# One more chunk of product g by seven small products, and a new table for the planner

## The chip, the cores and the metric

The kernel runs on one core of one Trainium2 chip. The metric is the device time of one execution in microseconds (us), the median of several runs. The kernel before takes 757.42 us (757.23 to 758.36, three runs).

## What is computed

One layer of a gated short-convolution mixer, all in float32: 1024 frames of 1024 features, an inner width of 2048. Cut to what matters:

```
u = rms_norm(x, pre_norm)
z, bg, cg, v = split(u @ w_in, 4)          # w_in 1024 x 8192
y = bg * causal_dwconv(cg * v, conv_w) * silu(z)      # 3 taps along the frames
out = x + rms_norm(y @ w_out, post_norm)   # w_out 2048 x 1024
```

Nearly all arithmetic is in the two matrix products.

## The kernel before, in words

**Tiles.** A float32 product is done as three float32r matmuls: an operand is split into a high and a low part, and lo x hi, hi x lo and hi x hi are summed in PSUM. The high part is a cast on ACT (names ending in h: wch, dwf1h), the low part a subtraction on VectorE (wcl, dwf1l), so each weight tile costs one operation on either. In the trace VectorE is DVE, ScalarE ACT, GpSimd POOL, SyncE SP.

**First product.** The 2048 inner columns go in 16 chunks c, and each chunk in two column pairs: p = 2c holds cg and v, p = 2c + 1 holds z and bg. A pair is multiplied by Strassen and Winograd's scheme with seven products a, b, c, e, d, f, g in place of eight; one is 4 x 3 matmuls of 128 x 512. POOL and VectorE form the sums of weight blocks that it needs (se, sc, sf, raw); the products gather in PSUM banks px, pv, py, from which ACT and VectorE take partial results (sna, snc, sne).

**Second level.** In the middle chunks the products b, f and g of both pairs together are done by the same scheme once more: seven small ones, a' to g', of 2 x 3 matmuls of 128 x 256 each (`deep_product`, L1472). Their weights are dwb, dwf, dwg with sums dsb, dsf, dsg; their results gather in banks px2b, pv2b, px2f, px2g and so on, and are added over by VectorE (for g: gs, then px). The left operands are u_g and others, made from u once. The second level of g overwrites a part of u_g; `restore_u` (L1723) reads that part from memory and splits it again, behind the last chunk that uses the second level.

**Which chunks.** `by_seven(z, c)` (L822) answers whether product z of chunk c is done by seven small ones: from chunk 2 up to but not including LAST[z] (L820), which was 16 for b, 15 for f and 14 for g. `late_conv(c)` (L946) follows from it: where g is done by seven, the convolution's last steps of chunk c (cv, then y, written out for the second product, and the sums s of it) are left for chunk c + 1.

**Second product.** y (y_d in memory), its sums (s_d) and w_out with its sums (t_d, tb_d) are multiplied in the same way from about 603 us on (names starting with o). Behind it stand the norm and the store.

**Order.** TensorE works in the order in which the code issues its matmuls. All other engines' order is made by a planner when the kernel is built: the class Plan records every operation, `deadlines` (L375) gives each a latest time, worked back from the matmul that needs it with an assumed length for each operation, and `arrange` (L428) plays the engines through and takes on each the ready operation with the earliest latest time; an idle VectorE may take an addition that was POOL's. PLAN (L28) holds the constants, and under "boost" a table that moves the latest time of single operations by their number. On the chip each engine then runs its row in that order and waits at the first operation whose input is missing.

Of the kernel before, what the change touches and what calls it, by code (L numbers as in the profile page):

```python
# [26 lines left out]
)  # L27
PLAN = {  # L28
    "end": 14.0,
    "psum": 3.0,  # L30
    "store": 6.0,
    "turns": 1,
    "apart": 11.0,
    "hard": 2.0,
    "lock": 0.3,
    "sum": 10.0,
    "early": 0.0,
    "gap": 0.5,
    "least": 1.0,
    "free": 40.0,  # L40
    "take": 11.0,
    "held": {"snc_1": 1.95},
    "ahead": {"sync": 24.0, "gpsimd": 18.0, "scalar": 11.0, "vector": 11.0},
    "busy": {"vector": 1.9, "scalar": 0.3, "gpsimd": -2.1},
    "slack": {"tensor": 1.0, "gpsimd": 0.8, "sync": 1.0, "scalar": 0.1, "vector": 0.1},
    "boost": {
# [38 lines left out]
    },  # L85
}
BY_BANK_DEEP = (("b", 0), ("b", 1), ("b", 2), ("f", 0), ("f", 2))
# [2 lines left out]
class View:  # L90
# [3 lines left out]
    def __init__(self, tile, steps, ids, dtype):  # L94
        self.tile, self.steps, self.ids, self.dtype = tile, steps, ids, dtype
# [111 lines left out]
    ((1, 2, 5, 6), 192),  # L207
)
LOW_PAGES = (3, 10, 11, 13, 15, 16, 5, 6, 8, 9)
U_SLOTS = (5, 4, 2, 6, 1, 3, 0, 0, 5, 2, 6, 4, 1, 3, 0, 5, 2, 6, 4, 1, 6, 3, 0, 4, 2, 5, 6, 1, 0, 3, 2, 4, 5, 6, 0, 4, 1, 5, 3, 6, 0, 2)  # L210


def gap(ctx, tc, name, size):
# [5 lines left out]
class Shelves:  # L219

    def __init__(self, ctx, tc):
        self.at, self.slots = {}, list(U_SLOTS)
        for n, (slots, room) in enumerate(U_LAYOUT):
            pool = ctx.enter_context(tc.tile_pool(name=f"up{n}", bufs=1))
            self.at.update({s: pool for s in slots})
            if n == 0:
                self.low = ctx.enter_context(tc.tile_pool(name="low_pages", bufs=1))
            gap(ctx, tc, f"room{n}", room)

    def tile(self, shape, dtype, tag, **kw):  # L230
        s = self.slots.pop(0)
        return self.at[s].tile(shape, dtype, tag=f"u{s}", **dict(kw, bufs=1))


# [19 lines left out]
class Plan:  # L254
# [35 lines left out]
    def call(self, engine, where, name, args, kw):  # L290
# [3 lines left out]
        op = Op()  # L294
# [26 lines left out]
        n = max([v.ids.size for v in (outs if where == "tensor" else outs + ins)], default=1)  # L321
        psum = any(v.tile.space == "psum" for v in outs + ins)
        two = sum(v.ids.size > 1 for v in ins) > 1
        if "dma" in name:
            op.dur, op.lat = self.ISSUE[where], 3.5 if where == "sync" else 7.5
            way = 2.0 if "accum_op" in kw else 1.5 if all(v.tile.space == "dram" for v in outs + ins) else 1.0
            op.move = n * 128 * 4 * way / 310e3
        elif where == "tensor":
            op.dur, op.lat = n / 2400 + 0.0135, n / 2400 + 0.2
        elif where == "vector":  # L330
            op.dur = 0.1 + n / 960 * (1 if psum or two else 0.55)
            op.lock = n > 8 and not psum
            op.lat = op.dur + 0.1
        elif where == "scalar":
            op.dur = 0.1 + n / 1200
            op.lat = op.dur + 0.16
        else:
            op.dur = 0.16 + n / 460 if n > 8 else 0.1
            op.lock = n > 8
            op.lat = op.dur + 0.1  # L340
# [328 lines left out]
def kernel(  # L669
# [22 lines left out]
    NC = CI // P  # L692
# [18 lines left out]
    psum = plan.pool(ctx.enter_context(tc.tile_pool(name="psum", bufs=8, space=bass.MemoryType.PSUM)), 8, "psum")  # L711
# [105 lines left out]
        wt[p, i] = [page(f"w{i}{h}_{p}", F32R) for h in "hl"]  # L817
        nc.scalar.copy(wt[p, i][0], source(p, i))

    LAST = {"b": NC, "f": NC - 1, "g": NC - 2}  # L820

    def by_seven(z, c):  # L822

        return {"b": DEEP, "f": DEEP_F, "g": DEEP_G}[z] <= c < LAST[z]

# [231 lines left out]
    xb = up.tile([P, TH, D], F32, tag="u", name="xb")  # L1057
# [724 lines left out]
    for n, slot in enumerate(slots):  # L1782
        if slot[2:]:
            z, i, c = slot
            deep_product(z, c, i)
            if (i, c) == ("e'", LAST[z] - 1) and LAST[z] < NC:
                restore_u(z)
# [25 lines left out]
        ahead = DEEP <= (p - (i == "a")) // 2 < DEEP_F and (i, p % 2) in (("d", 1), ("a", 0))  # L1813
# [320 lines left out]
```

## Time and profile before

| what | value |
|---|---|
| median of three runs | 757.42 us |
| the profiled execution | 758.85 us |
| its span in the trace | 757.1 us |
| first product, steady chunks | about 35.6 us each |
| first product ends, second product begins | 603.7 us |
| last matmul | about 750 us |

The profiled execution is 1.75 us longer than the span that the trace shows, and 1.4 us over the median. All L292 in the trace is one helper line through which every planned operation is issued (L356 after the change), so groups are told apart by their tiles: `wcl<-sc,wch` is the low part of weight c, made from sum sc and the high part.

### The profile page before, as it was taken

To read this page: it belongs to the slowest core of one execution; us is meant where nothing else is said; L and a number is where in the kernel's file an instruction comes from. 1 tells how busy PE (TensorE), PEld (TensorE's weight loads), DVE (VectorE), ACT (ScalarE), POOL (GpSimd) and SP (SyncE) were. 2 spreads that over 40 slices of the span, in tenths; PEclk is the share of its full clock that TensorE was granted. 3 is DMA by queue.
4 is the path that set the end of the run, shared out by engine and by line. 5 is a ranking of instruction groups with operands and counts; after the bars stand their busy time and mean duration, and the time that the engine had idled before them with its cause. 6 is when DMAs were issued, how large, how long until landed. Compare 5 with 4: busy or idle time off the path is not lost.

```text
span 757.1 us, 12810 instructions
## 1 busy us (share of the span) xinstructions
PE 745.2 (98%) x4320; PEld 660.0 (87%) x4320; DVE 677.9 (90%) x1022; ACT 458.7 (61%) x880; POOL 462.4 (61%) x416
## 2 busy tenths in 40 slices
PE   8999999999999999999999999999999999999996
PEld 7888889999999999989998988899888889889885
DVE  6899988999998988999999999898999999877994
ACT  7765588675656564655556565666553666565831
POOL 2509997889686777697788777685739100600421
PEclk9999999999999999999999999999999999999999
DMA  9313325244333548476949383928465999566842
GB/s 313 78 49 91 111 77 162 102 142 133 98 119 98 177 115 224 111 193 163 264 119 273 95 239 80 270 95 217 118 183 179 339 362 309 201 226 206 283 149 111
DMA packets 117137, 130.11 MB, mean 172 GB/s; under 512 B 7320, under 2 KB 74704, under 8 KB 116944
## 3 DMA queue, kind: packets, MB, share of 16 engines
q1 hardware_dynamic: 112560, 120.77, 50.1%
q0 software_dynamic: 4352, 8.39, 7.2%
q8 instruction: 34, 0.56, 0.3%
q14 instruction: 31, 0.25, 0.1%
q10 hardware_dynamic: 160, 0.14, 0.1%
HBM read 101.74 MB, written 44.30 MB: 193 GB/s over the span
## 4 chain that ended last, share of the span: by engine, by line
PE 75%; DVE 8%; POOL 6%; issue 4%; DMA 3%; ACT 3%; SPq 0%; POOLq 0%; DVEq 0%; ACTq 0%
PE px L292 29%; PE pv L292 12%; PE po_x L292 8%; PE px2b L292 4%; PE po_v L292 3%; PE pp L292 3%; PE px2f L292 3%; PE px2g L292 2%; PE pv2f L292 2%; PE pv2b L292 2%; PE pb_x L292 1%; POOL dsb L292 1%; DMA raw<-in_sc_w_in 1%; PE py L292 1%; PE py2b L292 1%
## 5 line engine op out<-in xcount | busy, mean ns | idle before, releaser
L292 PE MATMUL px<-u_a,wah 128*128 128x512 f32 x248 | 75.1, 383 | 0.0
L292 PE MATMUL px<-u_c,wch 128*128 128x512 f32 x248 | 74.9, 382 | 0.0
L292 PE MATMUL px<-u_d,wdh 128*128 128x512 f32 x248 | 74.9, 382 | 0.0
L292 PE MATMUL pv<-u_e,weh 128*128 128x512 f32 x248 | 74.7, 381 | 0.0
L292 ACT COPY beside<-raw 128x512 f32<-128x512 f32 x67 | 39.6, 591 | 34.2 <-DVE dwf2l L292 9.9
L292 PEld LDWEIGHTS px<-u_a,wah 128*128 128x128 f32 x248 | 46.5, 188 | 8.0
L292 PEld LDWEIGHTS px<-u_c,wch 128*128 128x128 f32 x248 | 46.5, 188 | 7.9
L292 PEld LDWEIGHTS pv<-u_e,weh 128*128 128x128 f32 x248 | 46.5, 188 | 7.7
L292 PEld LDWEIGHTS px<-u_d,wdh 128*128 128x128 f32 x248 | 46.5, 188 | 7.6
L292 DVE SCALAR_TENSOR_TENSOR cv<-gpad,cw,cv 128x1024 f32<-128x1024 f32 x32 | 49.8, 1557 | 3.3 <-ACT cv L292 3.2
L292 POOL TENSOR_TENSOR sf<-raw,sc 128x512 f32<-128x512 f32 x30 | 44.5, 1484 | 7.1 <-DVE sc L292 5.5
L292 PE MATMUL px<-u_c,wcl 128*128 128x512 f32 x124 | 47.9, 386 | 0.2 <-DVE wcl L292 0.2
L292 PE MATMUL px<-u_a,wal 128*128 128x512 f32 x124 | 47.8, 385 | 0.0
L292 PE MATMUL px<-u_d,wdl 128*128 128x512 f32 x124 | 47.7, 385 | 0.0
L292 PE MATMUL pv<-u_e,wel 128*128 128x512 f32 x124 | 47.5, 383 | 0.0
L292 POOL TENSOR_TENSOR sc<-se,raw 128x512 f32<-128x512 f32 x25 | 35.9, 1434 | 19.0 <-DVE se L292 10.4
L292 POOL TENSOR_TENSOR rs_post<-ve_post,minus_half 128x1 f32<-128x1 f32 x7 | 6.5, 941 | 65.9 <-DVE ve_post L292 65.9
L292 POOL TENSOR_TENSOR raw<-raw,raw 128x512 f32<-128x512 f32 x31 | 43.5, 1403 | 4.2 <-DVE se L292 3.8
L292 POOL TENSOR_TENSOR se<-raw,raw 128x512 f32<-128x512 f32 x22 | 32.2, 1463 | 18.7 <-DMA raw<-in_sc_w_in 9.4
L292 ACT COPY sna<-px 128x512 f32<-128x512 f32 x30 | 17.6, 585 | 34.4 <-PE px L292 34.4
L292 DVE TENSOR_TENSOR wcl<-sc,wch 128x512 fp32r<-128x512 f32 x31 | 33.8, 1089 | 5.0 <-ACT wch L292 5.0
L292 DVE TENSOR_TENSOR wel<-se,weh 128x512 fp32r<-128x512 f32 x31 | 32.3, 1043 | 0.0
(486 smaller groups left out, 2615.8 us busy)
## 6 DMA issues: line engine op xcount, KB each, us to landing
raw<-in_sc_w_in SPq DMA_DIRECT2D x128, 256.0 KB, 5.2
y_d<-cv SPq DMA_DIRECT2D x16, 512.0 KB, 2.7
s_d<-s SPq DMA_DIRECT2D x32, 256.0 KB, 4.9
t_d<-in_sc_w_out POOLq DMA_DIRECT2D x16, 512.0 KB, 8.5
tb<-in_sc_w_out SPq DMA_DIRECT2D x16, 256.0 KB, 3.5
t_d<-in_sc_w_out SPq DMA_DIRECT2D x16, 256.0 KB, 4.9
t_d<-t_d SPq DMA_DIRECT2D x16, 256.0 KB, 4.6
s<-y_d SPq DMA_DIRECT2D x16, 256.0 KB, 4.6
```

The source lines that it names most:

```text
L292: getattr(engine, name)(*(self.plain(a) for a in args), **{k: self.plain(a) for k, a in kw.items()})
```

## The change

**The product.** LAST["g"] goes from 14 to 15. Chunk 14's product g is no longer 2 x 12 matmuls of 512 columns but 7 x 6 of 256; `restore_u("g")` and the last plain g move a chunk on, and `late_conv(14)` becomes true.

**The planner.** Its assumed length of a matmul goes from n / 2400 + 0.0135 us to n / 2400 + 0.0088 for 512 columns and + 0.0079 for 256. Nine constants of PLAN and the boost table are new; with one more product by seven the operations of chunk 14 and behind it also have other numbers.

**Slots.** The memory slots of the u tiles, before a list in order of use, are now looked up by name; they are the same slots.

```diff
 PLAN = {
-    "psum": 3.0,
+    "psum": 2.53,
...
-    "apart": 11.0,
+    "apart": 10.4,
...
-    "sum": 10.0,
+    "sum": 9.37,
...
-    "gap": 0.5,
-    "least": 1.0,
+    "gap": 0.97,
+    "least": 0.35,
...
-    "take": 11.0,
+    "take": 9.19,
...
-    "ahead": {"sync": 24.0, "gpsimd": 18.0, "scalar": 11.0, "vector": 11.0},
+    "ahead": {"sync": 25.43, "gpsimd": 18.27, "scalar": 11.0, "vector": 9.92},
...
-    "slack": {"tensor": 1.0, "gpsimd": 0.8, "sync": 1.0, "scalar": 0.1, "vector": 0.1},
+    "slack": {"tensor": 0.96, "gpsimd": 0.75, "sync": 1.0, "scalar": 0.1, "vector": 0.1},
     "boost": {
-        0: -1.88, 1: 31.37, 2: -1.93, 4: 16.59, 5: 18.27, 6: 0.14, 20: 0.84, 21: 1.2, 22: 10.67, 27: -0.09,
...
+        0: -1.88, 1: 31.93, 2: -0.45, 4: 16.59, 5: 18.27, 6: 0.14, 20: 0.84, 22: 10.67, 23: 0.68, 26: 1.31,
...
-U_SLOTS = (5, 4, 2, 6, 1, 3, 0, 0, 5, 2, 6, 4, 1, 3, 0, 5, 2, 6, 4, 1, 6, 3, 0, 4, 2, 5, 6, 1, 0, 3, 2, 4, 5, 6, 0, 4, 1, 5, 3, 6, 0, 2)
+U_SLOTS = {
+    "u_a": 5, "u_b": 4, "u_c": 2, "u_e": 6, "u_d": 1, "u_f": 3, "xb": 0, "u_g": 0, "ou_a0": 5, "oy_a0": 2,
...
-        self.at, self.slots = {}, list(U_SLOTS)
+        self.at = {}
...
-        s = self.slots.pop(0)
+        s = U_SLOTS[kw["name"]]
...
         elif where == "tensor":
-            op.dur, op.lat = n / 2400 + 0.0135, n / 2400 + 0.2
+            op.dur = n / 2400 + (0.0088 if n == 512 else 0.0079 if n == 256 else 0.0135)
+            op.lat = n / 2400 + 0.2
         elif where == "vector":
...
-    LAST = {"b": NC, "f": NC - 1, "g": NC - 2}
+    LAST = {"b": NC, "f": NC - 1, "g": NC - 1}
```

The order that the planner makes differs from row 81 us on, on all four engines; VectorE has 8 rows more, ACT 5, POOL 1, and a number of additions have changed between POOL and VectorE. Three places follow. Numbers in names are of single tiles and differ between the two programs.

**First place: VectorE in chunk 14**, about 544 to 551 us before. s_13 is a sum of y of chunk 13, sna, snc and sne are partial results. Before:

```order
L292 TENSOR_TENSOR s_13_6276<-cv_6384,s_13_6276 128x512
L292 TENSOR_TENSOR cv_6384<-cv_6384,sna_6067 128x512
L292 TENSOR_TENSOR sne_6426<-px_6278,sne_6426 128x512
L292 SCALAR_TENSOR_TENSOR s_13_6365<-s_13_6276,s_13_6365 128x512
L292 TENSOR_TENSOR u_g<-ug,u_g 128x2x256
L292 SCALAR_TENSOR_TENSOR s_13_6522<-cv_6384,s_13_6365 128x512
L292 TENSOR_TENSOR snc_6396<-px2f_6461,snc_6396 128x256
L292 TENSOR_TENSOR wcl_6537<-sc_6391,wch_6441 128x512
L292 TENSOR_TENSOR snc_6396<-pv_6389,snc_6396 128x512
L292 TENSOR_TENSOR dwf1l_6553<-dsf_14_6477,dwf1h_6518 128x512
```

After:

```order
L356 TENSOR_TENSOR s_13_6342<-cv_6377,s_13_6342 128x512
L356 TENSOR_TENSOR wcl_6479<-sc_6370,wch_6410 128x512
L356 TENSOR_TENSOR sne_6424<-px_6279,sne_6424 128x512
L356 TENSOR_TENSOR snc_6388<-px2f_6458,snc_6388 128x256
L356 TENSOR_TENSOR dwf1l_6503<-dsf_14_6398,dwf1h_6485 128x512
L356 TENSOR_TENSOR snc_6388<-pv_6386,snc_6388 128x512
L356 TENSOR_TENSOR wel_6522<-se_6335,weh_6448 128x512
L356 SCALAR_TENSOR_TENSOR s_13_6481<-s_13_6342,s_13_6481 128x512
L356 TENSOR_TENSOR sna_6318<-px2b_6417,sna_6318 128x256
L356 SCALAR_TENSOR_TENSOR s_13_6546<-cv_6377,s_13_6481 128x512
```

The split u_g is gone from here (it stands 40 rows on, in chunk 15); wcl has moved up to the row behind the first product with s_13, and the two longer operations on s_13 (SCALAR_TENSOR_TENSOR) have moved behind dwf1l and wel.

**Second place: POOL in chunk 8**, about 319 to 331 us before. dsf_8 is a sum for the small products of f; its first half comes from one sf tile, its second from another; t and tb are sums of w_out. Before:

```order
L292 TENSOR_TENSOR dsb_8_3745<-dsb_8_3745,raw_01_3459 128x256
L292 TENSOR_TENSOR cv_3738<-cv_3738,sne_3557 128x512
L292 TENSOR_TENSOR t_13_3808<-tb_13_3703,tb_13_3697 128x256
L292 TENSOR_TENSOR dsf_8_3816<-sf_3755 128x256
L292 TENSOR_TENSOR t_13_3808<-t_13_3808,tb_13_3697 128x256
L292 TENSOR_TENSOR tb_13_3703<-tb_13_3703,t_13_3808 128x256
L292 TENSOR_TENSOR dsb_8_3852<-raw_01_3459,raw_01_3664 128x256
L292 TENSOR_TENSOR dsb_8_3852<-raw_01_3459,dsb_8_3745 128x256
L292 TENSOR_TENSOR dsf_8_3816<-dsf_8_3816,sf_3668 128x256
L292 TENSOR_TENSOR raw_10_3606<-raw_00_3621,raw_10_3606 128x512
```

After:

```order
L356 TENSOR_TENSOR dsb_8_3741<-dsb_8_3741,raw_01_3459 128x256
L356 TENSOR_TENSOR tb_13_3677<-tb_13_3677 128x256
L356 TENSOR_TENSOR cv_3734<-cv_3734,sne_3553 128x512
L356 TENSOR_TENSOR t_13_3806<-tb_13_3712,tb_13_3677 128x256
L356 TENSOR_TENSOR dsf_8_3796<-dsf_8_3796,sf_3645 128x256
L356 TENSOR_TENSOR t_13_3806<-t_13_3806,tb_13_3677 128x256
L356 TENSOR_TENSOR tb_13_3712<-tb_13_3712,t_13_3806 128x256
L356 TENSOR_TENSOR dsb_8_3862<-raw_01_3459,raw_01_3649 128x256
L356 TENSOR_TENSOR dsb_8_3862<-raw_01_3459,dsb_8_3741 128x256
L356 TENSOR_TENSOR dsf_8_3888<-sf_3645,sf_3744 128x256
L356 TENSOR_TENSOR dsf_8_3888<-sf_3645,dsf_8_3796 128x256
```

The second half of the first dsf (in place, from sf) stood seventh behind cv and stands second behind it now; its first half is no longer POOL's but VectorE's, and the addition raw is gone from here.

**Third place: VectorE in chunk 2**, about 121 to 125 us before. wdl is the low part of weight d, read beside its copy in a PSUM bank. Before:

```order
L292 TENSOR_TENSOR dsg_2_1328<-raw_11_1013 128x256
L292 TENSOR_TENSOR dwg0l_1337<-raw_11_859,dwg0h_1321 128x512
L292 TENSOR_TENSOR wdl_1346<-beside,wdh_1258 128x512
L292 TENSOR_TENSOR sna_1024<-pv2b_1219,sna_1024 128x256
L292 TENSOR_TENSOR sna_1213<-px2b_1101,sna_1213 128x256
L292 TENSOR_TENSOR snc_1077<-pv2f_1280,snc_1077 128x256
```

After:

```order
L356 TENSOR_TENSOR dwg0l_1318<-raw_11_830,dwg0h_1307 128x512
L356 TENSOR_TENSOR ufgl_deep<-beside,ufgh_deep 128x512
L356 TENSOR_TENSOR sna_1020<-pv2b_1215,sna_1020 128x256
L356 TENSOR_TENSOR sna_1209<-px2b_1099,sna_1209 128x256
L356 TENSOR_TENSOR snc_1078<-pv2f_1273,snc_1078 128x256
L356 TENSOR_TENSOR wdl_1364<-beside,wdh_1252 128x512
```

wdl has moved from ahead of the three additions from PSUM to behind them. On ACT the copy to the bank that wdl reads stands behind sne's copy and a cast ugch there, where it stood ahead of both.

More of the change, by code (lines that the diff above doesn't have):

```diff
@@ L209 @@
 LOW_PAGES = (3, 10, 11, 13, 15, 16, 5, 6, 8, 9)
-U_SLOTS = (5, 4, 2, 6, 1, 3, 0, 0, 5, 2, 6, 4, 1, 3, 0, 5, 2, 6, 4, 1, 6, 3, 0, 4, 2, 5, 6, 1, 0, 3, 2, 4, 5, 6, 0, 4, 1, 5, 3, 6, 0, 2)
+U_SLOTS = {
+    "u_a": 5, "u_b": 4, "u_c": 2, "u_e": 6, "u_d": 1, "u_f": 3, "xb": 0, "u_g": 0, "ou_a0": 5, "oy_a0": 2,
[4 rows of a table added]
+}
 def gap(ctx, tc, name, size):
```

136 rows, old and new, of tables (PLAN, U_SLOTS) are left out of this document.

## The prediction

> **What bounds the kernel now.** I read the page's first part, then what TensorE waits for, then stretches of the span, and last the single places where TensorE stands.
>
> ```profile
> span 757.1 us, 12810 instructions
> PE 745.2 (98%) x4320; PEld 660.0 (87%) x4320; DVE 677.9 (90%) x1022; ACT 458.7 (61%) x880; POOL 462.4 (61%) x416
> ```
>
> TensorE (PE) is busy in 98% of the span, so time can be gained in two ways only: fewer TensorE cycles, or fewer of the few holes. The holes come first, in the view of TensorE's waits (sum, count, longest, in us):
>
> ```profile
> PE px L292 <- DVE u_g L292: 1.1, 1, 1.1
> PE px2b L292 <- DVE dwb1l L292: 0.8, 2, 0.6
> ```
>
> Both are VectorE's (DVE) work that comes late: u_g in chunk 14, dwb1l in chunks 10 and 12. The view of stretches says where they lie, and how full VectorE is there (columns: length; then busy time and count of PE, PEld, DVE, ACT, POOL; clock, DMA share, GB/s):
>
> ```profile
> 280.00:480.00 200.00, 198.67 (x1217) 178.08 (x1217) 185.65 (x277) 117.05 (x225) 158.66 (x146) 1.00 0.66 177
> 540.00:560.00 20.00, 18.70 (x113) 16.33 (x112) 18.82 (x32) 11.02 (x22) 11.22 (x11) 1.00 0.69 198
> 560.00:600.00 40.00, 40.00 (x204) 34.37 (x203) 36.15 (x50) 21.36 (x38) 22.39 (x17) 1.00 0.64 210
> ```
>
> TensorE loses 1.30 us in 540 to 560 and 1.33 in 280 to 480, with the clock at 1.00. These are lower bounds: a record's end is modelled and lies behind the next one's start. So I count holes from start to start, against the undisturbed spacing, which the chain of waits shows (start, length, product, matmuls):
>
> ```profile
> 266.15 2.66 PE px L292 x12
> 268.81 0.69 PE px2b L292 x6
> ```
>
> 2.66/12 is 0.222 us for a matmul of 512 columns, 0.69/6 is 0.115 for one of 256.
>
> **Product g, arithmetic.** Chunk 14 did 2 x 12 matmuls of 512 for g; now it does 7 x 6 of 256: 24 x 0.222 = 5.32 us against 42 x 0.115 = 4.83. **Term 1: -0.5.** All of it lies on TensorE, so on the path.
>
> **Product g, the wait in chunk 14.** The timeline of TensorE and then of VectorE (start, length, engine):
>
> ```profile
> 545.73 0.39 PE L292 MATMUL px<-u_g,wgl 128*128 128x512 f32 x1
> 547.23 0.73 PE L292 MATMUL px<-u_g,wgh 128*128 128x512 f32 x2 [1.11 <-DVE u_g L292]
> ...
> 549.35 0.62 PE L292 MATMUL px<-u_g,wgh 128*128 128x512 f32 x2
> 550.16 0.47 PE L292 MATMUL px<-u_c,wcl 128*128 128x512 f32 x1 [0.19 <-DVE wcl L292]
> ```
>
> ```profile
> 545.97 1.21 DVE L292 TENSOR_TENSOR u_g<-ug,u_g 128x512 fp32r<-128x512 f32 x1
> 547.10 1.99 DVE L292 SCALAR_TENSOR_TENSOR s<-cv,s 128x512 f32<-128x512 f32 x1
> ...
> 549.34 0.68 DVE L292 TENSOR_TENSOR wcl<-sc,wch 128x512 fp32r<-128x512 f32 x1
> ```
>
> Plain g needs the first-level u_g back, which the second level had overwritten in part; that split (u_g) ends at 547.18 and TensorE starts at 547.23. The hole is 1.50 - 0.22 = 1.28. Behind it the sum s holds up wcl, and c starts 0.81 after two matmuls that take 0.44: 0.37. After the change u_g is restored some forty rows on and used only by chunk 15's g, and wcl stands behind one product, with both long operations on s behind it (front of this text, first place). I see nothing late in their stead: what follows is dwf1l, and it now also stands ahead of the s rows. A hole also slows the matmuls behind it by 0.1 (the record of two is 0.73 long behind the first hole, 0.62 further on). **Term 2: -1.85** (1.28 + 0.37 + 2 x 0.1).
>
> **The new order, holes at 331, 400 and 472.** The timelines of POOL, VectorE and TensorE in chunk 8:
>
> ```profile
> 328.72 0.73 POOL L292 TENSOR_TENSOR dsf<-dsf,sf 128x256 f32<-128x256 f32 x1
> ```
>
> ```profile
> 330.13 1.11 DVE L292 TENSOR_TENSOR dwf1l<-dsf,dwf1h 128x512 fp32r<-128x512 f32 x1 [0.71 <-ACT dwf1h L292]
> ```
>
> ```profile
> 330.30 0.61 PE L292 MATMUL px<-u_c,wch 128*128 128x512 f32 x2
> 331.30 0.38 PE L292 MATMUL px2f<-ufch_deep,dwf1l 128*128 128x256 f32 x1 [0.39 <-DVE dwf1l L292]
> ```
>
> TensorE stands from 330.30 + 0.44 to 331.30, 0.56, and 0.1 behind it. The cause is POOL's order: dsf's second half comes seventh behind cv, so the high half (ACT) and dwf1l come late. After the change dsf's first half is VectorE's and its second half is second behind cv on POOL (second place): four rows of 0.7 to 1.2 us fewer, more than the hole. **Term 3: -0.66.** In chunk 10:
>
> ```profile
> 397.68 1.22 DVE L292 TENSOR_TENSOR wcl<-sc,wch 128x512 fp32r<-128x512 f32 x1
> 398.83 0.68 DVE L292 TENSOR_TENSOR dwb1l<-beside,dwb1h 128x512 fp32r<-128x512 f32 x1
> ```
>
> ```profile
> 398.31 0.61 PE L292 MATMUL px<-u_a,wah 128*128 128x512 f32 x2
> 399.56 0.38 PE L292 MATMUL px2b<-ubch_deep,dwb1l 128*128 128x256 f32 x1 [0.64 <-DVE dwb1l L292]
> ...
> 472.51 0.38 PE L292 MATMUL px2b<-ubch_deep,dwb1l 128*128 128x256 f32 x1 [0.21 <-DVE dwb1l L292]
> ```
>
> The hole is 1.25 - 0.44 = 0.81, and 0.1 behind it. A product with s_9 stood ahead of wcl and dwb1l and moves behind both: that is one row of 0.7 to 1.2 us. Between nothing and 0.91 I take **-0.8 (term 4)**. In chunk 12 the same split waits, 0.21 against 0.64 by the records, so the hole is about 0.81 - 0.43 = 0.38, with 0.1 behind it; its s row also moves back. **Term 5: -0.47.** Smaller holes in these chunks (0.1 to 0.25 each, about 1.2 in all, read in the same timeline) I leave at 0, between -0.6 and 0: the order changes around them without a clear direction.
>
> **The new order, chunk 2.** Here a split moves back (third place): wdl was ahead of three additions from PSUM and is now behind them.
>
> ```profile
> 122.54 0.68 DVE L292 TENSOR_TENSOR wdl<-beside,wdh 128x512 fp32r<-128x512 f32 x1
> 123.14 0.41 DVE L292 TENSOR_TENSOR sna<-pv2b,sna 128x256 f32<-128x256 f32 x1
> ```
>
> ```profile
> 122.41 0.28 PE L292 MATMUL px2b<-ubdh_deep,dwb2h 128*128 128x256 f32 x1
> ...
> 123.10 0.27 PE L292 MATMUL px2f<-ufdh_deep,dwf2h 128*128 128x256 f32 x1
> 123.27 0.50 PE L292 MATMUL px<-u_d,wdl 128*128 128x512 f32 x1
> ```
>
> TensorE could start d at 123.10 + 0.115 = 123.21. The addition from px2b can't begin ahead of that product's end, 122.41 + 0.28 = 122.69; it and the next take about 0.33 from start to start (an addition of 0.41 follows at 123.14 + 0.33), so wdl starts at 123.35, ends at 124.03 and TensorE starts 0.05 later: a hole of 0.87 where 0.06 was, and 0.1 behind it. ACT's copy to the bank that wdl reads is also put behind two more operations there, which points the same way. Nothing covers this. Between 0 (these additions don't wait) and 1.4 (ACT is later still) **term 6: +0.9**.
>
> **The rest of the order.** Nearly every chunk from the third on has its rows permuted, and each can open a hole as those above. The old order had four of 0.4 us or more in 14 such chunks. The changed order gives some splits less slack by the same rows, and TensorE comes up to 3 us earlier to them. I take one of middle size, chunk 8's 0.66, less a little that the small holes give back: **term 7: +0.5**, between 0 and +2. Two plan items cost nothing: the slots by name are the same slots, and the head up to 80 us and the last 15 us keep their chain.
>
> **Sum.** -0.5 - 1.85 - 0.66 - 0.8 - 0.47 + 0.9 + 0.5 = -2.9. The profiled execution took 758.85 (span 757.1), 1.4 over the median 757.42 of the runs shown; it would come to 755.95, the median to **754.5**.
>
> **What the added work needs.** Seven small products want four splits and two pairs of additions more on VectorE, and three dsg on POOL. Groups of the trace, busy time and mean in ns:
>
> ```profile
> L292 DVE TENSOR_TENSOR wcl<-sc,wch 128x512 fp32r<-128x512 f32 x31 | 33.8, 1089 | 5.0 <-ACT wch L292 5.0
> L292 DVE TENSOR_TENSOR wdl<-beside,wdh 128x512 fp32r<-128x512 f32 x26 | 17.8, 684 | 3.8 <-ACT beside L292 3.0 <-POOL dsg L292 0.6
> L292 DVE TENSOR_TENSOR px<-px,gs 128x512 f32<-128x512 f32 x24 | 16.6, 692 | 0.3
> L292 DVE TENSOR_TENSOR dwg<-raw,dwg 128x256 fp32r<-128x256 f32 x12 | 11.7, 976 | 0.0
> ...
> L292 DVE TENSOR_TENSOR dwg1l<-dsg,dwg1h 128x512 fp32r<-128x512 f32 x12 | 9.7, 812 | 0.2 <-ACT dwg1h L292 0.2
> ```
>
> Three splits like dwg1l (2.44), dwg 0.98, two px 1.38, three additions of 0.41 (1.23), less two wgl at about wcl's 1.09 (2.18): +3.9 us. VectorE is idle 60 - 18.82 - 36.15 = 5.0 us in 540 to 600, so it fits, but with 1.1 to spare and TensorE there 2.3 earlier. That is the ground of the rivals.
>
> **Rivals.**
> *A, the order is better than I read it:* no hole in chunk 2 and none elsewhere: terms 1 to 5 and half the small holes, -4.3 - 0.6, **752.5**. For it: every hole of before is VectorE's order, and the order is what changes. Against: the wdl row. Chance 0.22.
> *B, the gain is used up:* VectorE has no room in chunks 14 and 15, so that term 2 stays only as far as 1.1 us of slack, and the holes at 331 to 472 reopen a few rows on: -0.5 - 1.1 + 0.9 = -0.7, **756.7**. For it: DVE fills 92% of 540 to 600. Against: POOL's late row in chunk 8 is a matter of order, not of load. Chance 0.18.
> *C, slower:* VectorE becomes the bound from 540 to 600. A split from two SBUF tiles beside a working POOL takes 1.22 (wcl at 397.68), alone 0.68 (wcl at 549.34); wdl, which reads a PSUM bank, has a mean of 684. With the four splits at 1.22 the addition is 4.88 + 1.38 + 1.23 - 2.18 = 5.3, and three more dsg stretch three other rows by 0.54: 6.9, which is 1.9 over the idle 5.0. Then TensorE ends the stretch 1.9 later than before; with terms 3 to 6 (-1.0) **758.3**. It decides from 6.0 us added. Against: POOL works only 33.6 of the 60 us there. Chance 0.09.
> [...]
> That the change doesn't do what it says is excluded by the order: the small products of chunk 14 stand there.
>
> **How the numbers follow.** Forecast 0.47 (753.3 to 755.9), A 0.22, B 0.18, C 0.09, 0.04 for 757 and above by other holes. The range goes from 752.2, below A, to 757.2, above B. A measurement can tell 0.2% (1.5 us) from no change: faster means under 755.9, the forecast and A with some of its edges, 0.74; same 0.17; slower 0.09.
>
> **What would show it.** In the profile of the changed kernel: no row of TensorE waiting for u_g; 42 small matmuls of g more and no px2f wait for dwf1l near 331; a wait for wdl near 124; TensorE idle in 280 to 480 well under 1.33; VectorE in 540 to 600 at 57 to 59 of 60. The forecast is wrong if new waits for splits between 130 and 530 sum to over 2 us, if wdl isn't waited for, or if TensorE waits in chunk 15.

## The result, and the profile after

The changed kernel takes **768.71 us** (median of four runs, 766.14 to 769.99); the kernel before, on the same chip, 757.50. The ratio is 1.0142 (1.0114 to 1.0169): 11 us slower, where 3 us less were forecast, and outside the range. The profiled execution took 768.57, its span is 766.8.

The page of the changed kernel begins:

```profile
span 766.8 us, 12865 instructions
PE 746.2 (97%) x4338; PEld 662.7 (86%) x4338; DVE 685.3 (89%) x1031; ACT 457.5 (60%) x883; POOL 469.5 (61%) x417
```

The span is 9.7 us longer and TensorE is busy only 1.0 longer: the time is in holes. What TensorE waits for (us in total, times, longest), the rows that matter:

```profile
PE pb_y L356 <- DVE oA_b L356: 4.4, 1, 4.4
PE px2g L356 <- DVE u_g L356: 1.6, 1, 1.6
...
PE px L356 <- DVE wdl L356: 1.3, 1, 1.3
PE px L356 <- DVE wcl L356: 1.3, 2, 0.8
PE px L356 <- ACT sna L356: 1.2, 2, 0.7
```

The u_g here is not the one of chunk 14: that wait is gone, as forecast. To see where each microsecond went, I take the start of product a in each column pair (the first matmul of px from u_a and wal) and the ends of the second product in both traces, and compare the stretches between. Chunk c runs from product a of pair 2c to that of pair 2c + 2; one without a hole takes 35.64.

| stretch | before | after | difference | forecast |
|---|---|---|---|---|
| chunk 2 | 35.34 | 38.67 | +3.33 | +0.9 |
| chunks 3 to 7 | 178.25 | 178.22 | 0 | |
| chunk 8 | 36.58 | 35.64 | -0.94 | -0.66 |
| chunk 9 | 35.69 | 37.41 | +1.72 | |
| chunk 10 | 37.36 | 38.13 | +0.77 | -0.8 |
| chunk 12 | 36.51 | 36.52 | 0 | -0.47 |
| chunks 14 and 15 | 78.63 | 76.95 | -1.68 | -2.35 |
| second product, first matmul to last | 146.83 | 153.41 | +6.58 | 0 |
| all others, the head among them | 165.14 | 165.09 | -0.05 | +0.5 |
| last matmul ends | 750.33 | 760.04 | +9.71 | -2.9 |

**The second product** holds two thirds of the loss. TensorE there, after (start, length, product, matmuls, and the wait ahead):

```profile
630.81 1.20 PE L356 MATMUL pb_y<-oB_b,oA_b 128*128 128x256 f32 x9
636.43 3.57 PE L356 MATMUL pb_y<-oB_b,oA_b 128*128 128x256 f32 x15 [4.42 <-DVE oA_b L356]
639.80 4.21 PE L356 MATMUL pb_x<-oB_b,oA_b 128*128 128x256 f32 x24
```

and before:

```profile
627.72 3.04 PE L292 MATMUL pb_y<-oB_b,oA_b 128*128 128x256 f32 x24
630.60 2.91 PE L292 MATMUL pb_x<-oB_b,oA_b 128*128 128x256 f32 x24
```

There is a hole of 4.6 us in pb_y, and the matmuls behind it are slow too: 24 took 4.21 where they took 2.91. The view of stretches gives the granted clock (seventh column, behind the five engines), in the slow stretch and right behind it:

```profile
636.40:642.60 6.20, 6.17 (x29) 6.17 (x30) 4.75 (x10) 2.38 (x5) 0.00 (x0) 0.50 0.87 268
642.60:646.00 3.40, 3.40 (x31) 3.40 (x31) 1.95 (x4) 0.73 (x2) 0.00 (x0) 1.00 0.98 331
```

For 6.1 us the clock is 0.50, which costs 2.95 us more (28 matmuls against their usual spacing). So the hole's price is 7.5. What made oA_b late begins 30 us earlier, on ACT and VectorE (the bracket is the idle time ahead and what ended it; "issue" means that the profile shows no releaser):

```profile
617.60 1.66 ACT L356 CAST oB_b<-ru_b 128x512 fp32r<-128x512 f32 x3 [11.08 <-issue]
...
629.03 1.57 ACT L356 COPY acc<-po_x 128x512 f32<-128x512 f32 x3 [4.04 <-DVE s L356]
...
635.03 0.62 ACT L356 CAST oA_b<-ry_b 128x512 fp32r<-128x512 f32 x1
```

```profile
618.25 0.69 DVE L356 TENSOR_TENSOR oB_b<-ru_b,oB_b 128x512 fp32r<-128x512 f32 x1 [3.69 <-ACT oB_b L356]
...
628.17 0.69 DVE L356 SCALAR_TENSOR_TENSOR s<-cv,s 128x512 f32<-128x512 f32 x1
...
635.68 0.69 DVE L356 TENSOR_TENSOR oA_b<-ry_b,oA_b 128x512 fp32r<-128x512 f32 x1
```

The first cast that ACT does there now writes oB2_b, which lives in slot 2; oy_a0 holds that slot until the 48 matmuls of product a that read it are done, the first half of this row:

```profile
606.63 21.60 PE L356 MATMUL po_x<-ou_a,oy_a 128*128 128x512 f32 x96
```

48 x 0.222 behind 606.63 is 617.3; in the built program this cast waits for TensorE's count at the end of these 48. ACT, in order, stands 11 us for it, and behind its casts VectorE stands 3.69. The three sums s of chunk 15 then end at 628.86 on VectorE, where they ended at 609.28 before. ACT's next row, the copy acc, waits 4.04 for the last of them, and the cast of ry_b, some ten rows further on, comes at 635.03. It feeds the oA_b that ends at 636.37. (SP issued the load of that ry_b late too, at 626.59 behind its store of the first s, where it issued it at 616.73 before. But it had landed at 630.13, 5 us ahead of its cast, so it isn't what TensorE waited for.) Before, the same engines stood so:

```profile
604.97 2.58 ACT L292 CAST oB_b<-B_b 128x512 fp32r<-128x512 f32 x4 [1.19 <-DMA B_b<-tb_d]
612.50 3.75 ACT L292 CAST oA_b<-ry_b 128x512 fp32r<-128x512 f32 x7 [2.24 <-DVE ry_b L292]
616.15 2.18 ACT L292 CAST oB_b<-ru_b 128x512 fp32r<-128x512 f32 x4
...
627.23 0.62 ACT L292 CAST oA_b<-ry_b 128x512 fp32r<-128x512 f32 x1
```

```profile
608.60 0.68 DVE L292 SCALAR_TENSOR_TENSOR s<-cv,s 128x512 f32<-128x512 f32 x1
```

The casts of oB2_b (from ru_b) stood behind those of oB1_b, oA1_b and oA2_b. oB2_b and oy_a0 are in slot 2 in both kernels; the order of those who use it had changed. The text ahead of the prediction has all slots the same, and they aren't: oB1_b, oB3_b and oA1_b were in 1, 3 and 0 and are in 3, 0 and 1 now, and tiles behind them moved with them.

**Chunk 2.** VectorE, ACT and TensorE, after:

```profile
122.20 0.69 DVE L356 TENSOR_TENSOR ufgl_deep<-beside,ufgh_deep 128x512 fp32r<-128x512 f32 x1 [0.40 <-ACT beside L356]
122.81 0.41 DVE L356 TENSOR_TENSOR sna<-pv2b,sna 128x256 f32<-128x256 f32 x1
...
123.82 0.69 DVE L356 TENSOR_TENSOR wdl<-beside,wdh 128x512 fp32r<-128x512 f32 x1
...
126.55 1.27 DVE L356 TENSOR_TENSOR dwg1l<-dsg,dwg1h 128x512 fp32r<-128x512 f32 x1
127.75 1.77 DVE L356 TENSOR_TENSOR dwg2l<-dsg,dwg2h 128x512 fp32r<-128x512 f32 x1
129.44 0.68 DVE L356 TENSOR_TENSOR ugcl_deep<-beside,ugch_deep 128x512 fp32r<-128x512 f32 x1
...
130.97 0.69 DVE L356 TENSOR_TENSOR u_g<-beside,u_g 128x512 fp32r<-128x512 f32 x1
```

```profile
123.19 0.59 ACT L356 COPY beside<-raw 128x512 f32<-128x512 f32 x1
...
130.15 0.78 ACT L356 COPY beside<-deepg 128x256 f32<-128x256 f32 x2 [2.06 <-DVE ugcl_deep L356]
```

```profile
124.57 0.50 PE L356 MATMUL px<-u_d,wdl 128*128 128x512 f32 x1 [1.29 <-DVE wdl L356]
...
131.72 0.49 PE L356 MATMUL px2g<-u_g,dwg0h 128*128 128x256 f32 x2 [1.64 <-DVE u_g L356]
```

Two holes, 1.46 and 1.80 from start to start. The first is the one forecast, bigger. wdl starts behind the three additions, but ACT's copy that it reads ends only at 123.78, so VectorE's order alone wouldn't have let it start earlier. The second hole wasn't foreseen. All of these copies use the one bank "beside", which ACT can fill again only when VectorE has read it. ugcl_deep, which reads it, stood ahead of dwg1l and dwg2l before and now stands behind both, and both took longer (1.27 and 1.77, where they took 0.97 and 0.68). ACT stands 2.06 for it before it copies what u_g needs.

### The profile page after: what moved, and what is told of

Read it like the earlier page. It is cut to its first block, busy times and chain, and to the rows that moved or that the text cites. A ratio compares the mean times of both kernels' runs of the same rounds, so it can differ in the third digit from the quotient of the medians.

```text
span 766.8 us, 12865 instructions
## 1 busy us (share of the span) xinstructions
PE 746.2 (97%) x4338; PEld 662.7 (86%) x4338; DVE 685.3 (89%) x1031; ACT 457.5 (60%) x883; POOL 469.5 (61%) x417
## 4 chain that ended last, share of the span: by engine, by line
PE 75%; DVE 10%; ACT 5%; DMA 4%; issue 4%; POOL 0%; SPq 0%; DVEq 0%; ACTq 0%; POOLq 0%
PE px L356 29%; PE pv L356 11%; PE po_x L356 8%; PE px2b L356 4%; PE pp L356 3%; PE po_v L356 3%; PE px2f L356 3%; PE px2g L356 3%; PE pv2f L356 2%; PE pv2b L356 2%; PE pf_x L356 1%; PE pb_x L356 1%; DVE cv L356 1%; PE py L356 1%; DMA s_d<-s 1%
## 5 line engine op out<-in xcount | busy, mean ns | idle before, releaser
L356 DVE SCALAR_TENSOR_TENSOR cv<-gpad,cw,cv 128x1024 f32<-128x1024 f32 x32 | 51.7, 1614 | 2.6 <-ACT cv L356 2.4
L356 POOL TENSOR_TENSOR sc<-se,raw 128x512 f32<-128x512 f32 x29 | 41.7, 1438 | 11.6 <-PE pv L356 3.6
L356 POOL TENSOR_TENSOR raw<-raw,raw 128x512 f32<-128x512 f32 x29 | 41.6, 1434 | 10.2 <-DVE se L356 10.2
L356 POOL TENSOR_TENSOR sne<-snc,sne 128x512 f32<-128x512 f32 x13 | 18.0, 1383 | 31.5 <-ACT snc L356 31.4
```

What stands on the lines that cost most here:

```text
L356: getattr(engine, name)(*(self.plain(a) for a in args), **{k: self.plain(a) for k, a in kw.items()})
```

## The experiments

All compare with the kernel before on the same chip (757.8 to 758.4 there).

**1. The product alone.** Kernel before with the one line; the table's numbers follow their operations.

```diff
-    LAST = {"b": NC, "f": NC - 1, "g": NC - 2}
+    LAST = {"b": NC, "f": NC - 1, "g": NC - 1}
```

> Only LAST['g'] is 15; the planner's constants, matmul lengths, slots and table are those of before, the table's numbers carried over to the same operations. Theory (the order is the cause: chunk 2 and the second product's start): no hole at 124 and 131, no 11 us wait of ACT near 606, time 755 to 759, some new waits of TensorE for wcl in chunks 14 and 15 being possible. Rival (the product is the cause: 4 us more of VectorE work and the later convolution make the second product's first operands late): the hole of 4 to 5 us near 630 stands here too, with the low clock behind it, time 763 or more.

Measured: 758.36 us, ratio 0.9994 (0.9976 to 1.0011). Chunk 2 takes 35.38. The second product takes 148.03, 1.20 more than before, with a hole of 1.18 at pb_y; chunks 14 and 15 take 77.29, 1.34 less. By the median the product is no loss, and no gain.

**2. The plan alone.** The changed kernel with g as before.

```diff
-    LAST = {"b": NC, "f": NC - 1, "g": NC - 1}
+    LAST = {"b": NC, "f": NC - 1, "g": NC - 2}
```

> LAST['g'] is 14 as before; constants, matmul lengths, slots by name and the table are those of the changed kernel (three table entries belong to operations that don't exist here and are left out). Theory (the order): 766 to 771, with holes of 1 to 2 us at 124 and 131 and one of 3 to 5 us near 630, behind an ACT that waits some 11 us for the slot of oB2_b. Rival (the product): 757 to 760, none of these beyond the ones of chunk 2.

Measured: 768.22, ratio 1.0141 (1.0112 to 1.0171): all of the loss, with the same waits; the second product takes 153.47.

```profile
PE pb_y L357 <- DVE oA_b L357: 4.6, 1, 4.6
PE px2g L357 <- DVE u_g L357: 1.6, 1, 1.6
```

**3. Slots in order of use.** The changed kernel, its slots taken from the old list as tiles are first used.

```diff
-        s = U_SLOTS[kw["name"]]
+        s = self.slots.pop(0)
```

> The changed kernel, but u slots are given in order of first use from the list, as before, not by name; the planned order is the same. oB2_b then takes slot 3 (free since product f of chunk 15) instead of 2 (held by oy_a0 until product a0 ends at 617). Theory (slot 2 is what ACT stands on for 11 us): ACT's first cast of oB2_b starts near 607 to 610, the hole near 632 and the clock dip behind it go, 5 to 8 us less: 761 to 764. Rival (late s sums of chunk 15 hold SyncE and so ry_b in any case): the hole stays over 2 us, 766 or more.

Measured: 767.85, ratio 1.0138 (1.0107 to 1.0168). The hole in pb_y fell to 0.86, and a new one stood 17 us on:

```profile
631.89 2.02 PE L350 MATMUL pb_y<-oB_b,oA_b 128*128 128x256 f32 x15 [0.69 <-DVE oA_b L350]
...
648.89 4.56 PE L350 MATMUL pb_x<-ox_b,oA_b 128*128 128x256 f32 x24 [3.90 <-ACT oy_c L350]
```

```profile
645.72 0.69 DVE L350 TENSOR_TENSOR oy_c<-ry_c,oy_c 128x512 fp32r<-128x512 f32 x1 [5.28 <-ACT oy_c L350]
...
648.07 0.68 DVE L350 TENSOR_TENSOR acc<-pb_x,acc 128x512 f32<-128x512 f32 x1
```

oB2_b has slot 1 in this run, not 3 as was expected. ACT's 11 us are gone, and with them 3.7 us of the hole in pb_y: that stand did hold TensorE up. But now another ACT cast (oy_c) waits for its slot, VectorE stands 5.28 behind it, and the addition that empties pb_x stands behind that. oy_c0 has the slot of oB2_b here, and that of oB1_b in the changed kernel; the last matmuls that read oB2_b (pb_v from ox_b) end at 644.99, and the cast starts at 645.07. So the exchange handed the wait on. It doesn't show that this order would be late under any slots.

**4. The head undone.** The changed kernel with the old matmul length in the first 75 us of the plan, and the old numbers for the operations below 900.

```diff
-            op.dur = n / 2400 + (0.0088 if n == 512 else 0.0079 if n == 256 else 0.0135)
+            op.dur = n / 2400 + (0.0135 if self.clock < 75.0 else 0.0088 if n == 512 else 0.0079 if n == 256 else 0.0135)
```

> The changed kernel, but for matmuls in the first 75 us of the plan (through chunk 2) the planner's old length, and for operations numbered below 900 the old table. Theory (the hole at 124 and that at 131 come from the order of ACT and VectorE in chunk 2): both fall under 0.5 us, 2.5 to 3.4 us less: 765 to 766.5, the hole near 632 unchanged. Rival (chunk 2 can't be served at TensorE's pace whatever the order, the earlier kernel having been helped by something else): holes of over 2 us in all stay, 767.5 or more.

Measured: 765.46, ratio 1.0101 (1.0071 to 1.013), 3.2 less than the changed kernel; the two intervals overlap a little. In the trace chunk 2 takes 36.15, 2.52 less: the hole at u_g is gone, that at wdl is 0.61, a little over the 0.5 expected.

**5 and 6. Another slot for oB2_b**, alone and with the head undone.

```diff
-"oB1_b": 3, "oB3_b": 0, ... "oB2_b": 2,
+"oB1_b": 0, "oB3_b": 2, ... "oB2_b": 3,
```

> The changed kernel; of the slots by name three entries differ: oB2_b gets slot 3 (free when u_f is), oB1_b slot 0, oB3_b slot 2 (oy_a0's). All else, the order too, stays. In the run with slots in order of use the hole at 632 shrank from 4.6 to 0.9 us, but ox_b and oy_c got other slots too and a hole of 4.1 us came up at 649. Theory (the place of one tile, oB2_b, is what the second product stumbles over, and the low clock comes with any hole this long): ACT's wait near 606 falls under 3 us, no hole over 1.5 us and no stretch with the clock under 0.9 behind 600; 6 to 7.5 us less than the changed kernel, 761 to 763. Rival (the planned order of the second product's loads and splits is late as a whole, and the hole only moves again): 765 or more.

> The changed kernel with the head undone and the three slots exchanged, both. Theory: the two add up, 3 and 7 us: 757.5 to 760, and what is left over the kernel before are the holes at 365 to 535, some 3 us, against the 2.4 that the product's own change saves there. Rival (they overlap, since a TensorE that comes earlier to the second product finds its operands later): 761 or more.

Measured: 771.13, ratio 1.0176 (1.0133 to 1.0218), and 767.29, ratio 1.0124 (1.0094 to 1.0155). ACT's 11 us at this cast went in both (it then stood 5.66 and 6.19 ahead of oA_b), the hole in pb_y fell to 1.99, and a hole came at pb_x behind oy_c and ou_c. That is the third experiment's once more: oy_c0 has oB2_b's slot, 3. Both times are the rivals', but for that reason; by the medians the head brings 3.8 with these slots too, so "they overlap" isn't what happened. Alone:

```profile
PE pb_x L356 <- ACT ou_c L356: 3.4, 1, 3.4
PE px L356 <- DVE wcl L356: 2.8, 2, 2.0
PE pb_y L356 <- DVE oA_b L356: 1.8, 1, 1.8
```

**7. The matmul length alone.** Kernel before, its table and constants, with the new length.

```diff
-            op.dur, op.lat = n / 2400 + 0.0135, n / 2400 + 0.2
+            op.dur = n / 2400 + (0.0088 if n == 512 else 0.0079 if n == 256 else 0.0135)
+            op.lat = n / 2400 + 0.2
```

> The kernel before; only the planner's assumed matmul length is the new one (0.0088 and 0.0079 in place of 0.0135), the old constants, table and product stay. Theory (a table of offsets fits the lengths that it was made with; change these and deadlines pass one another all along): many new holes, 763 or more. Rival (all deadlines shift alike, so the order hardly changes; what is slow is the new table): 756 to 760.

Measured: 764.46, ratio 1.007 (1.0045 to 1.0095); holes at wdl in chunk 2 (2.50) and at pb_y (2.46). A length that lies nearer to the trace made the plan worse. That the table's numbers are shifts against the old length is the likely reason; no run takes it apart.

**8 and 9. The second product's order undone**, alone and with the head. The changed kernel with the old numbers for the operations from 5250 on.

```diff
-         5248: 0.56, 5250: 1.84, 5255: -1.98, 5256: 3.42, 5258: -1.44,
+         5248: 0.56, 5258: -2.84, 5281: 1.84, 5283: 6.71, 5284: 0.33,
```

> Kernel after with the table's numbers for the operations of the second product and the end of chunk 15 (some 330 of about 800 operations from row 5250 to the end) taken from before, each carried over by the operation it belongs to. All slots stay by name. The cast of oB2_b then stands behind those of oA1_b and oA2_b on ACT, as in before, and the last three s of chunk 15 stand earlier on VectorE. Theory (the 7.2 us of the second product come from that order: ACT stands 11 us for slot 2, VectorE goes idle, the sums s come 17 us late, pb_y waits, and the clock falls): no wait of over 4 us of ACT between 606 and 618, the hole at pb_y about 630 to 636 falls from 4.6 to 1 to 2.7 us, and with it the slow matmuls behind it; 762.5 to 765 us. Rival (VectorE is short of time in that stage in any order, and the hole comes back at another place, as it did when only the slots were changed): 766 to 769.

> The same, and also the first 75 us of the plan with the old matmul length and the table's numbers of the operations below row 900 from before, as in the run that undid the head alone. Theory (two losses that add up, 3.2 us at the head and 4.5 to 7 in the second product): 758.5 to 761.5 us; what is left over before are the holes of chunks 8 to 13. Rival (the hole of the second product only moves, as in the run with head and slot 3): 764 to 767.

Measured: 764.95, ratio 1.0098 (1.0078 to 1.0118), and 763.98, ratio 1.0076 (1.0061 to 1.0092). ACT and TensorE in the eighth:

```profile
617.25 3.75 ACT L347 CAST oA_b<-ry_b 128x512 fp32r<-128x512 f32 x7 [4.09 <-DVE ry_b L347]
620.90 1.66 ACT L347 CAST oB_b<-ru_b 128x512 fp32r<-128x512 f32 x3
```

```profile
634.73 1.96 PE L347 MATMUL pb_y<-oB_b,oA_b 128*128 128x256 f32 x15 [1.89 <-DVE oA_b L347]
636.53 2.92 PE L347 MATMUL pb_x<-oB_b,oA_b 128*128 128x256 f32 x24
```

The casts of oA_b stand ahead again, the hole is 2.05, nothing behind it is slow, and the second product takes 148.48 where it took 153.41. The edit changes 128 numbers of the table, so it doesn't single out the cast. The median is 3.8 under the changed kernel's, at the upper end of the range expected; chunk 2 still takes 38.50. In the ninth both losses are gone from the trace (chunk 2 36.28, second product 148.03), but its median is 2.5 over the expected range. Its profiled execution reached product a of pair 1 at 30.73 us, where the changed kernel was at 28.81 and the fourth experiment, with the same head, at 28.63; without these 1.9 us it would lie near the range's upper end. The trace shows why: TensorE waited 1.12 for xa at 11.4 us, and from 13.4 to 16.6 us the granted clock was 0.50. The profiled execution of the fifth experiment began the same way (1.28, 0.50, 30.82). The other three executions of the ninth have no trace.

**10 to 12. New tables.** The old constants and the old length; a table in which, by the planner's own play-through, each split is ready 1.3 us ahead of its matmul where that can be had: with the product (10), without it as a control (11), and with the product by other numbers (12). In each, 102 to 109 numbers differ.

```diff
     "boost": {
...
-        241: -0.32, 247: 2.21, 264: 0.28, 286: 0.85, 303: -0.31, 306: 0.53, 311: -0.47, 339: -4.28, 347: -0.78,
+        241: -0.32, 247: 2.21, 264: 0.28, 286: 0.85, 303: -0.31, 306: 0.53, 311: -0.47, 337: -0.29, 339: -4.28,
+        343: 0.12, 347: -0.78, 386: 1.24, 403: 1.57, 426: -0.71, 428: 1.76, 431: 0.31, 433: 0.05, 440: 1.71,
...
```

> Kernel before with LAST g = 15, the old constants and the old matmul length, and a new table (109 numbers differ) in which every split stands so that, by the planner's own count, it is ready 1.3 us ahead of its matmul where that can be had. Theory (the loss lies only in rows that come too late for TensorE, and slack at those rows is what counts): the holes of 0.3 to 0.9 us in chunks 8 to 14 shrink from about 4 us to 1 to 2, that at pb_y stays at about 1.2; 753.5 to 756.0 us, where product alone with the old table was at 758.4 and before at 757.8. Rival (slack in the planner's count says little of the chip, since durations there vary with what the other engines do): 757 to 760, with other holes of the same sum.

> Control for the last: kernel before (LAST g = 14) with a table made in the same way, nothing else. Theory: the table is worth 2 to 3.5 us by itself, and the added product 0.5 us less the hole at pb_y of 1.2 that it brings; so 754 to 756, within 1 us of the run with the product. Rival (the product is worth its 2.4 us of chunk 14 once the order is right): this one 1.5 us or more slower than the run with the product.

> The product with another table that was made in the same way from other starts (104 numbers differ from the carried one). It tells what is luck of one table: theory 753.5 to 756.5, within 1 us of the first; rival, two tables of like slack differ by 2 us or more.

| | us | ratio to before (interval) | chunks 14 and 15 | second product |
|---|---|---|---|---|
| 10, product | **756.71** | 0.9981 (0.9967 to 0.9996) | 76.32 | 148.01 |
| 11, control | 756.90 | 0.9983 (0.9971 to 0.9995) | 76.75 | 146.66 |
| 12, product, second table | 759.46 | 1.0016 (1.0003 to 1.0029) | 80.11 | 147.52 |

The tenth and eleventh are a little faster than before, less than expected (both lie above their ranges), and alike; the twelfth is slower, so the rival "two tables of like slack differ by 2 us or more" was right. What sank it is one hole, in chunk 14:

```profile
PE px2b L303 <- DVE dwb L303: 2.1, 1, 2.1
```

The control is the telling one: with plain g in chunk 14 its matmuls from u_g follow one another with no wait,

```profile
546.73 0.39 PE L302 MATMUL px<-u_g,wgl 128*128 128x512 f32 x1
546.96 0.61 PE L302 MATMUL px<-u_g,wgh 128*128 128x512 f32 x2
```

and its chunks 14 and 15 take 0.43 more than those of the tenth; neither has a hole there. So the product itself is worth about 0.4 us there; the rest of what the change gained in chunk 14 a better order gives without it.

## Why the prediction was wrong, point by point

- **Term 1, the arithmetic (-0.5): right in size, but not the product's whole price.** The nearest measure is the 0.43 between experiments 11 and 10, both without a hole in these chunks. With the product there is a hole of 1.18 at pb_y in the second product under both tables (experiments 1 and 10), and without it none (before and 11). The sum had nothing for that.
- **Term 2, u_g and wcl in chunk 14 (-1.85): right.** Both waits are gone. Chunks 14 and 15 gained 1.68 where terms 1 and 2 said 2.35; a new hole of 0.69 at sna (at 535.1 us) is the difference.
- **Term 3, chunk 8 (-0.66): right in place; the size is partly luck.** The chunk has no hole under any version of the new order. But in experiment 1, which keeps the old order up to chunk 14, the same hole is 0.16 where it was 0.56 before.
- **Terms 4 and 5, chunks 10 and 12 (-0.8, -0.47): the waits for dwb1l went down as forecast (0.81 to 0.27, and 0.38 to none), the time didn't.** Other matmuls are late in the same chunks: in chunk 10 c waits 0.85 until ACT has emptied its bank (sna), behind a cast for which ACT had stood 4.28 (POOL's dsf), and there are 0.45 at dwg2l and 0.25 at dwf2l; in chunk 12 c waits 0.65 for wcl (start to start). The step priced the split that stood last, not what stands behind it.
- **Term 6, chunk 2 (+0.9): right in place and sign, too small.** The sum started two additions at the end of the px2b product; in the run all three stand behind a split that waits for ACT's copy, and the copy that wdl reads is late as well: 1.46. The second hole, 1.80 at u_g, comes from the same bank further on. The step saw that ACT's copy moved back and followed it only to the first matmul. The chunk lost 3.33; undoing the head gives 2.52 of it back (experiment 4).
- **Term 7, the rest (+0.5, up to 2): in the first product within its bounds.** Chunk 9 alone is +1.72: rows with s stand ahead of wcl there, as one did in chunks 10 and 12 before. It takes 37.36 or more in all eight traces of the new plan, so this one isn't chance.
- **The step that failed is a sentence of term 7:** "Two plan items cost nothing: the slots by name are the same slots, and the head up to 80 us and the last 15 us keep their chain." Nothing was said of 603 to 740 us, so the second product stood at 0 without a reason, and it cost 6.58 of the 9.71. (Nor are the slots the same; what that costs by itself no run shows.) The order that was read for three places was not read there, nor who holds the slots when. ACT's first cast had moved ahead of the matmuls that free its slot. Experiment 2 shows that the plan alone brings this loss. In experiments 3 and 5, where the cast needn't wait for that reader, the hole in pb_y falls from 4.58 to 0.86 and 1.99. The old order of these operations takes 4.93 of the 6.58 away with the slots as they are (experiment 8). Of the 1.65 that stay, 1.20 come with the product under the old table too (experiment 1).
- **A hole's price:** the prediction put 0.1 us behind each hole for slow matmuls. For holes of 2.15 us and more it is 1.6 to 2.95 us.
- **The rivals.** A and B fell. C, the slower one, fell as well, though its sign came: VectorE is busy 58.0 us in 540 to 600, within the 57 to 59 forecast, TensorE doesn't wait there, and the loss lies elsewhere.

```profile
540.00:560.00 20.00, 20.00 (x123) 17.94 (x122) 19.84 (x32) 11.76 (x23) 13.56 (x12) 1.00 0.62 172
560.00:600.00 40.00, 40.00 (x230) 35.52 (x229) 38.18 (x56) 21.31 (x39) 22.63 (x17) 1.00 0.60 199
280.00:480.00 200.00, 197.40 (x1208) 176.91 (x1207) 186.65 (x276) 115.00 (x220) 156.91 (x140) 1.00 0.67 179
```

The last row is the text's own test: TensorE idle "well under 1.33" in 280 to 480 is 2.60. A second one came true as well: the waits for splits between 130 and 530 (1.6 for u_g, 1.3 for wcl) sum to over 2 us. In these two traces the new order isn't better in the first product either.

**What stays open:** why chunks 8 to 13 keep 3.4 to 6.4 us of holes (over 6 x 35.64) under every table tried, and 8.7 in experiment 5. Part of it varies from one execution to the next under one order. Experiment 5 has the changed kernel's order throughout, and takes 222.58 there against 219.41: the wait for wcl in chunk 12 is 2.15 instead of 0.65, with low clock behind it. Experiment 1 has the order of before up to chunk 14, and takes 219.67 against 217.81. So differences of 2 to 3 us between single traces of that stretch prove nothing about an order.

## What to carry to other kernels

Where a planner's table changes, every stage has a new order: list, for each engine, the first operations that moved in each stage, and for each of them who frees the buffer that it writes; in the changed kernel ACT, in order, waited 11.08 us for a slot, VectorE stood 3.69 behind its casts, and SP issued its load of ry_b, behind a store of s, at 626.59 where it had been 616.73. Numbers that were fitted around a model are part of that model: correcting one constant without the others (experiment 7) cost 0.7%. And before a hole is blamed on an order, look at the same place in a second execution.

## What the runs showed of the hardware

**In these dense streams the price of a hole jumped between 2.05 and 2.15 us.** In the 14 traces, from 60 us on, all ten holes of 1.76 to 2.05 us are followed by one slow matmul at most (0.1 us); all ten of 2.15 to 4.74 us are followed by 9 to 28 matmuls at about twice their spacing (0.22 us for 256 columns in the trace after, where it is 0.115 otherwise), for 3.3 to 6.1 us, which costs 1.6 to 2.95 us more. The two sides of it, behind holes of 1.99 and 2.15 in experiment 5 (the clock is the seventh column):

```profile
641.00:643.00 2.00, 2.00 (x20) 2.00 (x19) 2.00 (x6) 0.00 (x0) 0.00 (x0) 1.00 0.89 307
```

```profile
466.60:469.00 2.40, 2.32 (x7) 1.91 (x8) 2.33 (x5) 0.63 (x2) 2.40 (x3) 0.66 0.88 255
469.00:471.50 2.50, 2.50 (x10) 2.04 (x10) 2.44 (x4) 1.80 (x3) 0.07 (x1) 0.64 0.49 175
```

So the hole of 2.15 us cost 3.9 and that of 2.05 (experiment 8) cost 2.15: by these two, an estimate, cutting one from 2.5 to 2.0 is worth more than the half microsecond. The length of one hole isn't all. In the head, where matmuls are sparser (TensorE is busy for 9.14 of the 10 us from 10 to 20 in the trace after, for all 40 from 60 to 100), waits of 1.12 and 1.28 us near 11.5 us were followed by the clock at 0.50 (experiments 9 and 5), one of 1.34 wasn't (experiment 8).

**In the traces before and after a split from two SBUF tiles took its usual time whenever POOL stood idle, and often longer beside POOL.** All 291 such splits of 128x512 that ran while POOL had no row took 0.67 to 0.69 us. Of the 175 that POOL's rows covered entirely, 127 took over 0.75, the longest 1.82; wcl at 439.13 in the trace after, with POOL's rows over 2.11 us of it, took 2.67. POOL's being busy isn't enough by itself: dwg2l of chunk 2 took 0.68 before (at 128.35) over rows of POOL with 256 columns, and 1.77 after (at 127.75) over two with 512. What makes the difference is not shown. It is part of the second hole there.
